# Operands loaded units ahead, gates moved to the end of their phase, attention steps lengthened, first two units interleaved

## The chip, the cores and the metric

The kernel runs on one core of one Trainium2 chip. The metric is the device time of one launch in microseconds (us), the median of several runs; less is better.

## The reference

One layer of a hybrid decoder, in float32, on a prompt of 1024 positions and on 8 sequences of 8 new tokens each (1088 rows together), with a model width of 2048:

```
proj = x @ w_in                                  # 2048 -> 84 blocks of 128 columns
gb, gc, h, z_c, q, k, v, z_a, gate_c, gate_a = split(proj)
y_c = silu(z_c) * gb * short_conv(gc * h)        # 3 taps along the sequence
o   = window attention of q over k, v            # 16 heads of 64, 4 key heads, window 128,
                                                 # ALiBi slopes, a sink logit for each head
y_a = silu(z_a) * o
merged = sigmoid(gate_c) * (y_c @ w_conv_out) + sigmoid(gate_a) * (y_a @ w_attn_out)
y = layer_norm(2**0.25 * x + merged @ w_out) * ln_g + ln_b
```

It also returns the last 128 rows of keys and values and the last two rows of the convolution's input, for the prompt and for each sequence (there after the cached ones).

## The kernel before, in words

**Units.** Activations lie transposed, as tiles of 128 features by T = 1088 rows, of which the first 64 are the new tokens. `w_in` and the two merge projections are multiplied by a 2 x 2 block scheme with seven products. Such a multiplication is cut into units (`unit`, L194): one unit takes a quarter-million weights (a tile `wr` of 128 x 4 x 512, 1024 KB) and 8 tiles of features, and makes two tiles of 128 x 1088. It has 7 products; a product is 4 slices of 6 matmuls (128 x 272), since every operand is kept as a pair: a value rounded to fp32r (ACT) and the rest (DVE subtraction), both made by `split` (L129). A product needs a weight operand (`ready`, L203; some are sums of two blocks) and four operand tiles, kept in a ring of 28 slots (`slot`, L142; 7 steps of 4). Its result goes from PSUM into a tile `c` (`take`, L222): a copy on ACT or an addition on DVE. After each slice `tick` (L92) advances a clock of steps; a unit is 28 ticks. Other PE work is put between the slices: `at` (L88) notes a function for a tick.

**Operands.** `operands` (L148) loads the four quarters of four pairs of feature tiles (16 loads of 272 KB), makes the sums on DVE (L174, L176, L183, L186) and splits all 28 operand tiles (`xa`, `xb`, `xm` in the profile). Each set replaces the one before it in the ring.

**Stages.** (1) 42 units a0 to a41 with the upper half of x's features, their results spilled to DRAM (`pd`). (2) 42 units b with the lower half, which add to the spilled result: two for keys and values (b0, b1), eight for queries and attention gates (b2 to b9; `queries`, L336, and `attend`, L441), eight gates (b10 to b17) beside the attention of the new tokens (`sample`, L508), then eight times two conv units (b26 to b41; `conv`, L605) with one gate each (b18 to b25). `gate` (L462) is a unit, a sigmoid of its whole result and a store to `sgd`. (3) 8 units with conv outputs (m0_0 to m0_7) and 8 with attention outputs (m1_0 to m1_7), multiplied by the gates (`sg`) and added up (`cmo`); the profile names both psm_0 to psm_7. (4) The product with `w_out` in plain matmuls (`o`): 5 row blocks by 4 column blocks by 16 k-steps, then 4 row blocks, with residual and layer norm.

**Attention.** 64 steps (`Step`, L357; 8 pairs of heads by 8 blocks), one in 15 ticks, lie in the slices from b3 on. A step has four parts at fixed ticks after its start (L446 to L449): `load`, 14 ticks later `scores` (matmuls `sc`, then the softmax on DVE and ACT), 11 ticks after that `turn` (four transposes `pt`, then a split into `pp`), 9 ticks after that `output` (matmuls `po`). All three take a PSUM bank of the two tagged `ax` (`aux`, L126). The new tokens' attention has such ticks too (L589 to L593).

**Order.** PE's instructions are chained in program order (`in_order`, L99). On the other engines, and on SP, which issues all DMAs, the framework's planner orders the instructions when the program is built, by times that it simulates; it may pull an instruction ahead of earlier ones as far as its data and buffers allow. `tc.keep_in_program_order` holds one instruction behind whatever was traced before it on its engine. A pool's memory can be used by a later pool when the tiles that lay there are released.

**Output.** After the last merge unit, five `w_out` tiles are loaded into the units' weight buffers (`early`, L692); then the units' pool is closed and the pool `out` takes its memory, with the other raw weights (`wraw`), the raw merged rows (`yr`), the split rows of the new tokens (`ms`) and 8 more slots. `Out.load` (L748) loads the residual rows.

Of the kernel before, what the change touches and what calls it, by code (L numbers as in the profile page):

```python
# [50 lines left out]
def tile_hybrid_step(  # L51
# [8 lines left out]
    def pool(name, bufs=1, space=None, stack=None):  # L60
        kw = {} if space is None else {"space": space}
        if space is not DRAM:
            kw["reuse_waits"] = "tile"
        return (stack or ctx).enter_context(tc.tile_pool(name=name, bufs=bufs, **kw))
# [4 lines left out]
    ps = pool("ps", space=PSUM)  # L69
# [78 lines left out]
    def operands(stage, name, sources):  # L148

        out = [[None] * 4 for _ in range(7)]
        raws = []
        for k, (top, bottom) in enumerate(sources):
            raw = stage.tile([P, 2, T], F32, name=f"xr{name}{k}", tag=f"xr{k}")
            raws.append(raw)
        for h in range(2):
            for r in range(2):
                for raw, src in zip(raws, sources):  # L160
                    c = slice(h * HALF, (h + 1) * HALF)
                    nc.sync.dma_start(raw[:, r, c], src[r][:, c])
        left, right = slice(0, HALF), slice(HALF, T)

        def put(i, src):
            for k in range(4):
                o = slot([2, HALF], F32R, f"x{name}{i}_{k}")
                split(o[:, 0], o[:, 1], src(k))
                out[i][k] = o


        t2 = []
        for k, x in enumerate(raws):
            nc.vector.tensor_sub(x[:, 0, right], x[:, 1, right], x[:, 0, right])  # L174
            t = stage.tile([P, HALF], F32, name=f"t{name}{k}", tag=f"t{k}")
            nc.vector.tensor_add(t, x[:, 0, right], x[:, 0, left])  # L176
            t2.append(t)
        put(0, lambda k: raws[k][:, 0, left])
        put(1, lambda k: raws[k][:, 1, left])
        put(2, lambda k: t2[k])  # L180
        put(3, lambda k: raws[k][:, 0, right])
        for k, x in enumerate(raws):
            nc.vector.tensor_sub(x[:, 0, left], x[:, 1, right], t2[k])  # L183
        put(4, lambda k: raws[k][:, 0, left])
        for k, x in enumerate(raws):
            nc.vector.tensor_sub(x[:, 1, left], x[:, 1, left], t2[k])  # L186
        put(5, lambda k: raws[k][:, 1, left])
        put(6, lambda k: raws[k][:, 1, right])
        return out
# [5 lines left out]
    def unit(name, src, x, c, add):  # L195

        raw = upool.tile([P, 4, 512], F32, name=f"wr{name}", tag="wr", bufs=2)
        nc.sync.dma_start(raw.rearrange("p a b -> p (a b)"), src)
        a11, a21, a12, a22 = (raw[:, i] for i in range(4))
        s = upool.tile([P, 2, 512], F32, name=f"ws{name}", tag="ws", bufs=1)  # L200
# [14 lines left out]
        acc_a, acc_c, acc_b = sums(f"ps{name}")  # L215
# [17 lines left out]
        for i in range(7):  # L233
# [13 lines left out]
            take(*after[i])  # L247


    with ExitStack() as st:  # L250
        stage = pool("stage", stack=st)

        idle = stage.tile([P, HALF], F32, name="idle", tag="t0")
        nc.vector.memset(idle, 0.0)
        t = aux("idle")
        for i in range(WARM):
            matmul(t, idle[:, 0:P], idle[:, 0:512], start=True, stop=True)
        x0 = operands(stage, "a", [(xt[k], xt[k + 8]) for k in range(4)])
        for p in range(len(PAIRS)):
            c = upool.tile([P, 2, T], F32, name=f"ca{p}", tag="c", bufs=2)  # L260
            unit(f"a{p}", win[p, 0], x0, c, False)
            nc.sync.dma_start(pd[p], c)
        x1 = operands(stage, "b", [(xt[k], xt[k + 8]) for k in range(4, 8)])
# [31 lines left out]
    def project(p):  # L295
        c = upool.tile([P, 2, T], F32, name=f"cb{p}", tag="c", bufs=2)
        nc.sync.dma_start(c, pd[p])
        unit(f"b{p}", win[p, 1], x1, c, True)
        return c

    ap = pool("attn", stack=keep)
    kv_ready = {}
# [54 lines left out]
    class Step:  # L357
# [9 lines left out]
        def load(self):  # L367
# [6 lines left out]
            nc.sync.dma_start(self.ks[:, : self.nk].bitcast(F32), ksd[self.g][:, self.lo : self.lo + self.nk])  # L374
            self.vc = ap.tile([P, 2, P], F32R, name=f"vt{n}", tag="vt", bufs=2)
# [65 lines left out]
    def attend(j):  # L441
        t0 = max(clock[0] + 1, attend_from[0])
        for blk in range(NB):
# [4 lines left out]
            at(t + 25, s.turn)  # L448
            at(t + 34, s.output)  # L449
# [3 lines left out]

    with ExitStack() as st:
        sp = pool("heads", stack=st)
        for i in range(2):
            keys_values(i, project(KV + i), sp)
# [4 lines left out]
    def gate(d):  # L462
        c = project(GT + d)
        nc.scalar.activation(c, c, AF.Sigmoid)
        nc.sync.dma_start(sgd[d], c)


    with ExitStack() as st:
# [39 lines left out]
        def sample(g, hb):  # L508
# [5 lines left out]
            sbias = sp.tile([32, L], F32, name=f"sbias{n}", tag="sbias")  # L514
            nc.sync.dma_start(sbias, sbias_d[:, g])
            kt = sp.tile([HD, NH, L], F32, name=f"skt{n}", tag="skt")
# [5 lines left out]
            va = sp.tile([P, NH, HD], F32, name=f"sva{n}", tag="sva")  # L522
# [431 lines left out]
```

## Time and profile before

| | us |
|---|---|
| median of 3 runs | 2820.47 |
| lowest and highest | 2820.05, 2821.55 |
| the profiled execution | 2821.96 |
| its span, from the first instruction to the last | 2820.1 |
| mean granted TensorE clock | 0.971 |

The profile is of one execution. A row of a group reads: line, engine, operation, output<-inputs by the program's names, shapes, count; then busy us and the mean ns of one; then the idle time of the engine just before such instructions and what ended it. PE is TensorE's matmuls, PEld its weight loads, DVE VectorE, ACT ScalarE, SPq the queue of SP that issues DMAs. In the list of waits a row says who waited for whom, us in total, how many times, and the longest. In the timeline a row begins with its start and its duration, and ends, in brackets, with the idle time before it. L110 and L113 are the helpers of all matmuls and transposes, L130 and L131 the two halves of `split`, L227 the additions into `c`.

### The profile page before, as it was taken

What the parts mean: (1) busy time and instruction counts of PE and PEld (TensorE: products, weight loads), DVE (VectorE), ACT (ScalarE), POOL (GpSimd) and SP (SyncE); (2) the same over time, 40 slices, a digit from 0 to 9 for tenths busy, and PEclk for the clock granted to TensorE, in tenths of its full rate; (3) what the DMA queues carried; (4) which work ended last, traced back from release to release, by engine and by line L of the source; (5) the groups of instructions that cost most, each with busy time, mean ns of one, the idle gap of its engine ahead of it and who ended that gap; (6) DMA issues with size and microseconds to landing.
All of it is one profiled execution on the core that took longest, in us unless ns stands there. A gap on an engine that the chain in (4) does not pass through costs nothing.

```text
span 2820.1 us, 47966 instructions
## 1 busy us (share of the span) xinstructions
PE 2660.1 (94%) x19426; PEld 2563.4 (91%) x19426; DVE 1756.9 (62%) x3311; ACT 1072.5 (38%) x2050; POOL 0.2 (0%) x4
## 2 busy tenths in 40 slices
PE   6999999999999989899999999999899999699998
PEld 5999999999999989798999999889899999578886
DVE  7444444444445767687877777777875866433736
ACT  4323323233234445456545444443433422322221
POOL 0000000000000000000000000000000000000000
PEclk8999999999999999899999999999999999899999
DMA  5222222222223456654544444433454366823533
GB/s 202 93 109 108 95 108 107 99 106 106 102 106 118 164 172 198 189 190 149 189 132 155 162 155 143 156 131 129 172 198 165 128 216 214 263 91 109 186 116 105
DMA packets 165026, 411.53 MB, mean 146 GB/s; under 512 B 23186, under 2 KB 75410, under 8 KB 136868
## 3 DMA queue, kind: packets, MB, share of 16 engines
q1 hardware_dynamic: 164804, 408.46, 42.6%
q8 instruction: 153, 2.51, 0.4%
q14 instruction: 69, 0.57, 0.1%
HBM read 290.88 MB, written 119.48 MB: 146 GB/s over the span
## 4 chain that ended last, share of the span: by engine, by line
PE 76%; DVE 12%; DMA 5%; ACT 4%; issue 3%; SPq 0%; DVEq 0%; ACTq 0%
PE o L110 13%; DVE cb L227 2%; DVE wb L131 1%; DMA sg<-sgd 1%; PE pt L113 1%; PE psm_4a L110 1%; PE psm_2a L110 1%; PE psm_5a L110 1%; DMA cmo<-cmd 1%; PE sc L110 1%; ACT p L412 1%; PE psm_0a L110 1%; DVE xm L131 1%; PE po L110 1%; PE psm_6a L110 1%
## 5 line engine op out<-in xcount | busy, mean ns | idle before, releaser
L110 PE MATMUL o<-wo,m 128*128 128x512 f32 x1344 | 319.9, 393 | 0.2 <-DVE r L767 0.2
L110 PEld LDWEIGHTS o<-wo,m 128*128 128x128 f32 x1344 | 254.1, 189 | 55.6 <-issue 0.6
L131 DVE TENSOR_TENSOR wa<-wra,wa 128x512 fp32r<-128x512 f32 x210 | 145.2, 692 | 214.7 <-ACT wa L130 214.7
L130 ACT CAST wb<-wrb 128x512 fp32r<-128x512 f32 x210 | 129.8, 618 | 270.6 <-PE psb3b L110 8.3
L130 ACT CAST wa<-wra 128x512 fp32r<-128x512 f32 x210 | 130.9, 624 | 175.9 <-PE psa0b L110 2.4
L131 DVE TENSOR_TENSOR wo<-wraw,wo 128x512 fp32r<-128x512 f32 x107 | 73.1, 686 | 146.0 <-ACT wo L130 138.4
L131 DVE TENSOR_TENSOR wb<-wrb,wb 128x512 fp32r<-128x512 f32 x210 | 143.7, 684 | 8.6 <-ACT wb L130 8.1
L130 ACT CAST wo<-wraw 128x512 fp32r<-128x512 f32 x107 | 66.2, 621 | 214.4 <-PE o L110 197.1
L131 DVE TENSOR_TENSOR wa<-wsa,wa 128x512 fp32r<-128x512 f32 x84 | 58.1, 692 | 115.2 <-ACT wa L130 115.2
L113 PE MATMUL pt<-ident,p 128*128 128x128 f32 x240 | 47.8, 305 | 50.9 <-ACT p L412 49.8
L130 ACT CAST wb<-wsb 128x512 fp32r<-128x512 f32 x84 | 52.0, 619 | 96.9 <-PE psb18a L110 6.5
L113 PEld LDWEIGHTS pt<-ident,p 128*128 128x128 f32 x240 | 29.9, 148 | 62.0 <-ACT p L412 61.8
L130 ACT CAST wa<-wsa 128x512 fp32r<-128x512 f32 x84 | 52.3, 623 | 78.9 <-issue 76.9
L405 ACT ACTIVATE p<-p,nm 128x256 f32<-128x256 f32 (+1 forms) x128 | 62.4, 488 | 40.9 <-DVE nm L397 40.6
L676 DVE TENSOR_TENSOR cm<-cm,sg 128x544 f32<-128x544 f32 x64 | 46.1, 721 | 49.1 <-DMA sg<-sgd 29.8
L131 DVE TENSOR_TENSOR pp<-pt,pp 128x512 fp32r<-128x512 f32 (+1 forms) x64 | 41.8, 653 | 55.8 <-ACT pp L130 55.7
L131 DVE TENSOR_TENSOR wm<-wrm,wm 128x512 fp32r<-128x512 f32 x80 | 55.0, 687 | 33.3 <-ACT wm L130 33.2
L130 ACT CAST wm<-wrm 128x512 fp32r<-128x512 f32 x80 | 49.8, 622 | 65.7 <-PE psm_0b L110 4.8
L412 ACT ACTIVATE p<-p,den 128x256 f32<-128x256 f32 (+1 forms) x128 | 56.4, 488 | 38.8 <-DVE den L410 38.0
L110 PE MATMUL o<-wo,ms 128*128 128x512 f32 x128 | 40.2, 396 | 28.0 <-DVE ms L131 25.4
L131 DVE TENSOR_TENSOR wb<-wsb,wb 128x512 fp32r<-128x512 f32 x84 | 57.7, 687 | 2.3 <-ACT wb L130 1.9
L110 PEld LDWEIGHTS o<-wo,ms 128*128 128x128 f32 x128 | 24.1, 191 | 33.9 <-issue 27.8
(1089 smaller groups left out, 6582.5 us busy)
## 6 DMA issues: line engine op xcount, KB each, us to landing
pd<-ca SPq DMA_DIRECT2D x42, 1088.0 KB
cb<-pd SPq DMA_DIRECT2D x42, 1088.0 KB
wra<-in_win SPq DMA_DIRECT2D x42, 1024.0 KB
wrb<-in_win SPq DMA_DIRECT2D x42, 1024.0 KB
wraw<-in_wo SPq DMA_DIRECT2D x123, 256.0 KB
sgd<-cb SPq DMA_DIRECT2D x16, 1088.0 KB
sg<-sgd SPq DMA_DIRECT2D x64, 272.0 KB
qt<-qd SPq DMA_DIRECT2D x128, 128.0 KB
```

Of the source, the lines that this page charges most:

```text
L110: in_order(nc.tensor.matmul(*args, **kw))
L113: in_order(nc.tensor.transpose(*args))
L130: nc.scalar.copy(hi, raw)
L131: nc.vector.tensor_sub(lo, raw, hi.bitcast(F32))
L227: nc.vector.tensor_add(dst, dst, val)
L405: nc.scalar.activation(p[:, e, :nk], p[:, e, :nk], AF.Exp, bias=nm[:, e : e + 1], accum_out=den[:, e : e + 1],)
L412: nc.scalar.mul(p[:, e, :nk], p[:, e, :nk], den[:, e : e + 1])
L676: nc.vector.tensor_mul(c[:, f, hs], c[:, f, hs], sg)
```

## The change

*Start and operands.* `operands` becomes a class with separate parts: `load_all` (four loads for each quarter, held in program order), `combine` (the first eight sums), and `step(i)`, which makes the operands of product i only. A unit becomes a generator, `products`, that stops after each product; `enter` runs a set's seven steps, each followed by that product of one or more units. The first two units run side by side with one set, their weights loaded between the quarters, in a PSUM pool of their own of eight banks.

*Hand-overs.* The second set (`x1`) is loaded and combined after unit a36, and its steps are interleaved with b0. The set for conv outputs is loaded and combined before the last three gates, that for attention outputs after the fifth merge unit; both are entered step by step.

*Order of gates.* Nine gates lie beside the new tokens' attention, one after every second conv pair, three after all. A gate's sigmoid is made in two halves.

*Attention.* `turn` comes 16 ticks after `scores`, `output` 10 after `turn`; values and the attention gate are loaded 28 ticks after the step's start. The new tokens' steps come later by 4 to 8 ticks, with two buffers for three of their tiles.

*Output.* `sg` has three buffers. Raw weights and raw merged rows of the output lie in a pool of their own (`mq`), opened after m1_0; the early weights go. The residual loads are held in program order.

```diff
+    class Operands:
+        def load(self, r, c, tag):
+            out = []
+            for k, src in enumerate(self.sources):
+                t = self.stage.tile([P, HALF], F32, name=f"x{tag}{self.name}{k}{r}{c}", tag=f"x{tag}{k}")
+                tc.keep_in_program_order(
+                    nc.sync.dma_start(t, src[r][:, c * HALF : (c + 1) * HALF])
+                )
+                out.append(t)
+            return out
+
+        def load_all(self, between=lambda: None):
+            self.b11 = self.load(0, 0, "a")
+            between()
+            self.b21 = self.load(1, 0, "d")
+            between()
+            self.b22 = self.load(1, 1, "c")
+            self.b12 = self.load(0, 1, "b")
+
+        def combine(self):
+            self.t3, self.t2 = self.b12, self.b22
+            for k in range(4):
+                nc.vector.tensor_sub(self.t3[k], self.t2[k], self.t3[k])
+                nc.vector.tensor_add(self.t2[k], self.t3[k], self.b11[k])
+            self.b22 = None
...
+        def step(self, i):
+            if i == 2 and self.b22:
+                self.combine()
+            if i == 4:
+                for k in range(4):
+                    nc.vector.tensor_sub(self.t3[k], self.b22[k], self.t2[k])
+            if i == 5:
+                for k in range(4):
+                    nc.vector.tensor_sub(self.b21[k], self.b21[k], self.t2[k])
+            self.put(
+                i,
+                (lambda: self.b11, lambda: self.b21, lambda: self.t2, lambda: self.t3,
+                 lambda: self.t3, lambda: self.b21, lambda: self.b22)[i](),
+            )
+            if i == 3:
+                self.b22 = self.load(1, 1, "a")
+
+    def enter(x, *units):
+        for i in range(7):
+            x.step(i)
+            for u in units:
+                next(u)
...
+        x0.load_all(first_weights)
+        s1 = fpool.tile([P, 2, 512], F32, name="wsa1", tag="idle")
+        both = [
+            products(f"a{p}", raws[p], x0.x, c[p], False, (acc[2 * p], acc[2 * p + 1], acc[2 * p + 1]), (None, s1)[p])
+            for p in range(2)
+        ]
+        enter(x0, *both)
...
+    for p in range(2, len(PAIRS)):
+        c = upool.tile([P, 2, T], F32, name=f"ca{p}", tag="c", bufs=2)
+        unit(f"a{p}", win[p, 0], x0.x, c, False)
+        nc.sync.dma_start(pd[p], c)
+        if p == 36:
+            x1.load_all()
+            x1.combine()
...
-            at(t + 25, s.turn)
-            at(t + 34, s.output)
+            at(t + 28, s.load_values)
+            at(t + 30, s.turn)
+            at(t + 40, s.output)
...
-        nc.scalar.activation(c, c, AF.Sigmoid)
+        for f in range(2):
+            nc.scalar.activation(c[:, f], c[:, f], AF.Sigmoid)
...
-            at(t0 + 6, lambda: scores(0))
-            at(t0 + 9, lambda: scores(2))
-            at(t0 + 13, softmax)
-            at(t0 + 20, turn)
-            at(t0 + 25, output)
+            at(t0 + 10, lambda: scores(0))
+            at(t0 + 13, lambda: scores(2))
+            at(t0 + 17, softmax)
+            at(t0 + 26, turn)
+            at(t0 + 33, output)
...
+        gate(8)
...
-            gate(8 + ct)
+            if ct % 2:
+                gate(9 + ct // 2)
...
+    x = branch(0)
+    for d in range(13, 16):
+        gate(d)
...
+    for b, w in enumerate((wc, wa)):
+        for i in range(8):
+            c = upool.tile([P, 2, T], F32, name=f"cm{b}_{i}", tag="c", bufs=2)
+            u = products(f"m{b}_{i}", w[i], x.x, c, False)
+            if i == 0:
+                enter(x, u)
+            else:
+                for _ in u:
+                    pass
+            if (b, i) == (1, 0):
+                st.close()
+                mq = pool("oraw", side="right")
+            merged(b, i, c)
+            if (b, i) == (0, 4):
+                nxt = branch(1)
+        x = nxt
...
-            nc.sync.dma_start(self.r[n][: self.rows], self.x[:, n * 512 : (n + 1) * 512])
+            tc.keep_in_program_order(
+                nc.sync.dma_start(self.r[n][: self.rows], self.x[:, n * 512 : (n + 1) * 512])
+            )
```

`branch(b)` makes a set from `yd`, loads it and combines it. `merged` is the loop of gates and sums that stood in the merge before.

More of the change, by code (lines that the diff above doesn't have):

```diff
@@ new lines, in enter, with unit, products @@
+    def enter(x, *units):
[3 more added lines that the diff above has]
+                next(u)
+        for u in units:
+            assert next(u, None) is None
+    def unit(*args):
+        for _ in products(*args):
+            pass
+    def products(name, src, x, c, add, accs=None, s=None):
+        if len(src.shape) == 3:
+            raw = src
+        else:
+            raw = upool.tile([P, 4, 512], F32, name=f"wr{name}", tag="wr", bufs=2)
+            nc.sync.dma_start(raw.rearrange("p a b -> p (a b)"), src)
@@ L247, in unit, with first_weights @@
             take(*after[i])
-    with ExitStack() as st:
-        stage = pool("stage", stack=st)
-        idle = stage.tile([P, HALF], F32, name="idle", tag="t0")
+            yield
+    st = ExitStack()
+    stage = pool("stage", stack=st, side="right")
+    x0 = Operands(stage, "a", [(xt[k], xt[k + 8]) for k in range(4)])
+    with ExitStack() as first:
+        ps0 = pool("ps0", space=PSUM, stack=first)
+        fpool = pool("first", stack=first, side="right")
+        acc = [ps0.tile([P, 2, 512], F32, name=f"first{i}", tag=f"first{i}") for i in range(4)]
+        idle = fpool.tile([P, 2, 512], F32, name="idle", tag="idle")
         nc.vector.memset(idle, 0.0)
-        t = aux("idle")
         for i in range(WARM):
[L257 to L263, printed above, removed]
+            matmul(acc[0][:, 0], idle[:, 0, 0:P], idle[:, 0], start=True, stop=True)
+        c = [upool.tile([P, 2, T], F32, name=f"ca{p}", tag="c", bufs=2) for p in range(2)]
+        raws = []
+        def first_weights():
+            p = len(raws)
+            raws.append(upool.tile([P, 4, 512], F32, name=f"wra{p}", tag="wr", bufs=2))
+            nc.sync.dma_start(raws[p].rearrange("p a b -> p (a b)"), win[p, 0])
+        x0.load_all(first_weights)
[5 more added lines that the diff above has]
+        enter(x0, *both)
+        for p in range(2):
+            nc.sync.dma_start(pd[p], c[p])
+    ps = pool("ps", space=PSUM)
+    x1 = Operands(stage, "b", [(xt[k], xt[k + 8]) for k in range(4, 8)])
+    for p in range(2, len(PAIRS)):
[5 more added lines that the diff above has]
+            x1.combine()
     keep = ExitStack()
@@ new lines, in tile_hybrid_step, with branch, merged @@
+    mp = pool("merge", side="right")
+    st = ExitStack()
+    stage = pool("mstage", stack=st, side="right")
+    def branch(b):
+        x = Operands(stage, f"m{b}", [(yd[8 * b + k], yd[8 * b + k + 4]) for k in range(4)])
+        x.load_all()
+        x.combine()
+        return x
+    x = branch(0)
+    for d in range(13, 16):
+        gate(d)
+    def merged(b, i, c):
+        for f in range(2):
+            for h in range(2):
+                hs = slice(h * HALF, (h + 1) * HALF)
+                sg = mp.tile([P, HALF], F32, name=f"sg{b}_{i}_{f}{h}", tag="sg", bufs=3)
+                nc.sync.dma_start(sg, sgd[i + 8 * f][:, b, hs])
+                nc.vector.tensor_mul(c[:, f, hs], c[:, f, hs], sg)
+                if b:
+                    sg = mp.tile([P, HALF], F32, name=f"cmo{i}_{f}{h}", tag="sg", bufs=3)
+                    nc.sync.dma_start(sg, cmd[i][:, f, hs])
+                    nc.vector.tensor_add(c[:, f, hs], c[:, f, hs], sg)
+        nc.sync.dma_start((mgd if b else cmd)[i], c)
```

119 lines of the change are left out of this document (35 added, 84 removed).

## The prediction

> **What bounds the kernel now.** I read the page's head first, then the list of what TensorE (PE) waited for, then the busy times in the stretches between the kernel's stages.
>
> ```profile
> span 2820.1 us, 47966 instructions
> PE 2660.1 (94%) x19426; PEld 2563.4 (91%) x19426; DVE 1756.9 (62%) x3311; ACT 1072.5 (38%) x2050; POOL 0.2 (0%) x4
> ```
>
> PE sets the time, so only its gaps and its slow spells can be won: 160 us without a matmul. The list of waits says who ended them:
>
> ```profile
> engine line waited for: us in total, times, longest us
> PE pt L113 <- ACT p L412: 49.8, 24, 4.5
> PE o L110 <- DVE ms L131: 25.4, 2, 24.6
> PE psa0a L110 <- ACT wa L130: 13.4, 1, 13.4
> PE sps L110 <- DMA skt<-in_ckt: 7.4, 1, 7.4
> PE pko L113 <- DVE o L435: 3.1, 1, 3.1
> PE psb3a L110 <- DVE cb L227: 2.8, 1, 2.8
> PE sc L110 <- DMA qt<-qd: 2.5, 1, 2.5
> ```
>
> A unit is 7 products of 24 matmuls, and a product at full clock takes 3.01 us (row below), so a unit takes 21.1 us; 843.7 us for the 40 units a1 to a40 says 21.09.
>
> ```profile
> 88.65 3.01 PE psa2a L110 x24
> ```
>
> The stretches end where the units end. Columns: us, then busy us (instructions) of PE, its weight loads, DVE and ACT, POOL, the granted clock, the DMA share.
>
> ```profile
> 0.00:55.50 55.50, 30.03 (x174) 26.99 (x175) 47.59 (x76) 26.58 (x43) 0.20 (x4) 0.75 0.61 218
> 55.50:899.20 843.70, 843.70 (x6722) 843.70 (x6722) 383.49 (x560) 256.33 (x440) 0.00 (x0) 1.00 0.27 104
> 899.20:927.30 28.10, 23.49 (x171) 23.27 (x170) 26.86 (x43) 21.36 (x39) 0.00 (x0) 0.88 0.32 117
> 992.50:2029.40 1036.90, 968.34 (x7449) 946.25 (x7448) 784.93 (x1765) 508.66 (x1072) 0.00 (x0) 0.97 0.49 161
> 2029.40:2066.40 37.00, 24.51 (x170) 23.11 (x170) 34.85 (x56) 19.20 (x31) 0.00 (x0) 0.82 0.54 201
> 2193.00:2221.00 28.00, 23.26 (x170) 23.04 (x170) 27.34 (x44) 21.55 (x38) 0.00 (x0) 0.88 0.36 117
> 2221.00:2394.00 173.00, 170.00 (x1345) 168.79 (x1343) 115.46 (x179) 51.71 (x89) 0.00 (x0) 1.00 0.63 202
> 2394.00:2430.00 36.00, 11.20 (x43) 8.85 (x42) 8.83 (x16) 5.40 (x12) 0.00 (x0) 0.67 0.90 302
> 2430.00:2808.70 378.70, 373.77 (x1670) 307.87 (x1670) 196.33 (x367) 97.94 (x174) 0.00 (x0) 1.00 0.42 133
> ```
>
> What each loses beyond its units: **start** 55.5 - 21.1 = 34.4; **first hand-over** (a41) 28.1 - 21.1 = 7.0; **attention and gates** (39 units) 1036.9 - 968.3 = 68.6 idle, and 3% of 1036.9 = 31 by the clock, together 99.7; **second hand-over** (m0_0) 37.0 - 21.1 = 15.9; **third** (m0_7, m1_0's operands) 28.0 - 21.1 = 6.9, and 173.0 - 8 x 21.09 = 4.3 in the eight units behind it; **out hand-over** 36.0 less 43 matmuls at 378.7 / 1670 = 0.227 us, so 26.2. In all 194.5 us; the change touches each of these.
>
> **The change, part by part.** *Start.* Today 16 operand loads go ahead of the first weights, and the operands of all seven steps are split before the second weight:
>
> ```profile
> GB/s 0 189 396 335 382 380 402 373 370 418 426 421 273 11 0 0 0 0 0 0 15 295 353 107 308 335 251 335 221 65 322 228 412 389 48 0 0 6 458 289
> 10.14 1.10 SPq L198 DMA_DIRECT2D wra<-in_win  x2
> 27.24 0.60 DVE wa L131
> 27.84 2.54 DVE xa L131 x4
> ```
>
> The first row is the DMA rate in slices of 1.5 us: about 0.39 MB/us from 1.5 us on. The new order is four quarter loads (B11, 1.11 MB), weight 0 (1.05), B21, weight 1, B22, B12. They land near 4.4, 7.0, 9.9, 12.6, 15.5 and 18.3 us, plus half a microsecond. The first matmul comes near 8.5 (after one cast and one subtraction of 0.6 us), the second unit's near 14, and four products bring PE to about 23-24. From 16.7 (first B12 tile) DVE has the eight sums, 20 operand splits and eight later sums at 2.54/4 = 0.635 (22.9 us), 10 weight splits and 4 weight sums at 0.60 (8.4) and 6 additions into c at 0.635 (3.8): 35.1 us, so it is done at 52 and the last two products at 56.5. Today unit a1 ends at 76.6. Gain 20. Below 53 it can't end (12 products behind 17 us), and with DVE's present disorder it would be 65: gain 12 to 24. Two units share one operand step, so DVE has 6 us of matmuls to hide 4 to 7.5 us in, instead of 3; that is the cover, and DVE is late next.
>
> *The first hand-over.* The loads are not what is late:
>
> ```profile
> 30.41 15.12 SPq L162 DMA_DIRECT2D xrb<-in_xt  x15
> ```
>
> The planner has already put them at 30 us. The 28 splits wait for slots that a41 frees product by product. DVE's work between the end of a41's first product and b0's last is 28 splits and 8 sums (36 x 0.635 = 22.9) and about 16 us of the two units' own, 39 us in 36 us of products. So some 3 us stay, whatever the order: gain 4 (0 to 7). The moved loads now issue behind a36's store: 16 issues at about 0.6 us are 9 us of SP's queue and 4.45 MB are 11.4 us of DMA. What queues behind them is a38's weights, needed a unit (21 us) later; without that cover it would cost up to 10 us. The eight sums moved with them (5 us of DVE) fall where DVE is busy 383 of 844 us: nothing.
>
> *Second and third.* The three last gates, 63 us, now hide the loads of conv outputs, which today start after the last gate's work has begun:
>
> ```profile
> 2016.25 11.67 SPq L162 DMA_DIRECT2D xrm<-yd  x16
> ```
>
> With loads and first sums gone the same 3.5 us of DVE excess stays: 15.9 - 3.5 = 12 gained (0 to 15.9). At the third, the loads come four units early; of 6.9 + 4.3 = 11.2 us some 5 stay, as the merge adds DVE work: 6 gained (0 to 11). The third `sg` buffer goes with this.
>
> *Attention.* A turn waits for the softmax. One such step:
>
> ```profile
> 1442.60 0.65 PE L110 MATMUL sc<-kt,qt 128*128 128x256 f32 x4
> 1444.60 2.42 PE L110 MATMUL psb27c<-xb,wb 128*128 128x272 f32 x18
> 1446.85 0.63 PE L110 MATMUL po<-pp,vt 128*128 128x256 f32 x4
> 1450.04 0.57 DVE L435 TENSOR_TENSOR o<-po,ot 64x128 f32<-64x128 f32 x2
> 1456.10 1.30 PE L113 MATMUL pt<-ident,p 128*128 128x128 f32 x4 [4.10 <-ACT p L412]
> 1485.19 0.95 PE L113 MATMUL pt<-ident,p 128*128 128x128 f32 x4 [2.11 <-ACT p L412]
> 1487.05 3.64 PE L110 MATMUL psb18a<-xb,wb 128*128 128x272 f32 x18
> ```
>
> Scores start at 1442.60 and PE could turn 9.4 us later, but the softmax takes 13.5. The turn moves from 11 to 16 ticks behind the scores, a tick being 6 matmuls (3.01/4 = 0.75 us): 3.8 us, and another 0.5 for the next step's scores now ahead of it. The longest wait is 4.5, so of 49.8 us at most 24 x 0.2 = 5 stay if the softmax comes no later. The clock comes back with them: after a wait of 2.11 us 18 matmuls took 3.64 us against 2.42. The sample scores come 4 ticks later, taking 3.0 of the 7.4 us. What stays: sample cache 4.4, pko 3.1, the first step's 2.8 and 2.5, together 13; 6 for turns behind DVE bursts or a PSUM bank; 6 of clock: 25 of 99.7, gain 74. Values and szt are now loaded 28 ticks into a step but 12 ticks (9 us) ahead of their use. All eight conv steps now lie beside attention, so DVE has its 785 us in some 960: 82% instead of 76%. Two half sigmoids for one cost more table loads:
>
> ```profile
> L464 ACT ACT_TABLE_LOAD x14 | 18.0, 1283 | 0.3
> ```
>
> With an exponential between the halves that is two more loads for each of 16 gates, 41 us of ACT at most, which is busy 509 of 1037 and hides it; in one softmax it is 1.3 us of the 4.3 won. Bounds of this stage: 20 (DVE keeps the chain late) to 90.
>
> *Out hand-over.* Today the last merged block waits behind residual loads that the planner pulled ahead, and everything for the output waits behind that block's store:
>
> ```profile
> 2394.91 6.18 DMA r<-in_x_p
> 2401.15 5.67 DMA cmo<-cmd
> 2418.64 10.42 DMA yr<-mgd
> ```
>
> Pinned residuals take the 6.2 out; raw operands and raw weights lie in a pool of their own on the other side, and may come during m1. The first 14 of 16 k-steps don't need the last block and are 14 x 14 matmuls x 0.227 = 44 us of cover for its store. What can be late next is `ms`, still in the pool that takes the units' memory. I take 6 of 26.2 left: gain 20 (0 to 25).
>
> Sum: 20 + 4 + 74 + 12 + 6 + 20 = **136 us**. The profiled execution took 2821.96 us, 1.9 beyond its span, and the median of the runs is 2820.47: 2822 - 136 = 2686, on the median's scale **2684**.
>
> **The rivals.**
> *DVE stays behind in attention.* For: at 1442 to 1455 the softmax is late because conv's work stands ahead of it in DVE's order, and conv steps now come in pairs with no gate between. Against: on the whole DVE has a fifth of the time free. Half of the 74 lost: 2684 + 37 = **2721**.
> *The output still waits for the last block's store*, through `ms`: 20 lost, **2704**.
> *Early operands do nothing*: all three operand hand-overs are DVE's work, not loads, as the row at 30.41 shows for the first. 4 + 12 + 6 = 22 lost: **2706**.
> *Short waits leave the clock alone.* By the row at 1487.05 a wait of 2.1 us already costs 1.2 us more. If only waits of over 3.4 us did, the 6 us of clock that I leave in attention and some 2 elsewhere would go: **2676**.
> The Trainium skill ("TensorE: Matmul & The Clock Gate", the section on the HAM clock gate) has that rule: the clock halves after about one idle window of 3.4 us. By that rule the time would be this rival's; the row at 1487.05 speaks against it.
> *Slower: the PSUM bank.* Scores, turn and output share two `ax` banks. A turn now takes the bank of the output that ran 5 ticks before it (today no bank is taken again within 9 ticks): 3.8 us, and 1 for that output and the scores between. In the step shown the bank was free 3.8 us after the output began (1450.61 - 1446.85); one of the later ones is
>
> ```profile
> 1392.30 0.40 PE L110 MATMUL po<-pp,vt 128*128 128x256 f32 x2
> 1397.14 0.58 DVE L435 TENSOR_TENSOR o<-po,ot 64x128 f32<-64x128 f32 x2 [0.23 <-ACT ot L432]
> ```
>
> 5.4 us, so 0.6 of wait. It decides when every one of 64 steps loses 136/64 = 2.1 us, with 1 of clock in it, that is, when banks come free some 6 us after the output on average; at 7 us it is 64 x (2.2 + 1.2) = 218 lost against 136 won: **2902**.
>
> **How the numbers follow.** Forecast 0.57, DVE 0.17, output 0.10, clock 0.07, no help at hand-overs 0.05, bank 0.04. The forecast alone, by its unknown costs, lies between 2645 and 2715. The range is **2645 to 2735**: the cases at 2676, 2704, 2706 and 2721 lie in it, with room for DVE's to cost a third more than half; out of it fall the bank (0.04) and some 0.05 at either end. A measurement of this kernel tells 0.2% (5.6 us) from no change. All cases but the bank lie over 80 us on the fast side; milder forms of the bank case could meet zero. Faster 0.95, same 0.01, slower 0.04.
>
> **What would show it.** Right: a2 starts near 57; PE's waits on ACT p L412 sum to under 8 us, and the attention stretch has a clock of 0.99; m0_0 and m1_0 take under 26 us; the first output matmul comes within 8 us of the last merge product. Wrong: a wait of pt on DVE o (the bank); den late although pt was moved (DVE); o on ms for over 15 us (the store); many waits of PE on c's additions at L227's successor, which would put DVE ahead of PE as the bound.

## The result and the profile after

| | kernel before | changed kernel |
|---|---|---|
| median, four runs each | 2821.01 us | 2730.85 us |
| lowest and highest | 2820.05, 2826.04 | 2727.61, 2732.11 |
| ratio, 95% interval | | 0.9675 [0.9658, 0.9692] |
| profiled execution, span | 2820.1 | 2728.5 |

The change takes 3.25% off. The forecast was 2684, so two thirds of the 136 us came: the span fell by 91.6. The head of the page after:

```profile
span 2728.5 us, 48044 instructions
PE 2635.7 (97%) x19426; PEld 2546.2 (93%) x19426; DVE 1751.0 (64%) x3311; ACT 1076.7 (39%) x2070; POOL 0.2 (0%) x4
```

To see where they came from, I divided both spans at the same units: where a2 begins, and where b0, b25, m0_0 and m1_7 end. These are the busy times by stretch, first of the kernel before (columns as in the prediction):

```profile
0.00:76.40 76.40, 50.93 (x340) 47.89 (x341) 57.16 (x90) 32.98 (x54) 0.20 (x4) 0.82 0.52 187
76.40:948.60 872.20, 867.57 (x6892) 867.16 (x6891) 416.47 (x615) 278.13 (x479) 0.00 (x0) 1.00 0.28 106
948.60:2029.40 1080.80, 1012.24 (x7801) 990.15 (x7800) 816.57 (x1813) 526.84 (x1106) 0.00 (x0) 0.97 0.49 163
2066.40:2394.00 327.60, 319.86 (x2521) 318.43 (x2519) 219.25 (x338) 111.67 (x193) 0.00 (x0) 0.99 0.56 181
2394.00:2820.10 426.10, 384.98 (x1713) 316.72 (x1712) 212.59 (x400) 103.64 (x187) 0.00 (x0) 0.96 0.45 146
```

and then of the changed kernel:

```profile
0.00:70.20 70.20, 53.53 (x340) 49.43 (x341) 52.37 (x84) 32.93 (x54) 0.20 (x4) 0.88 0.42 153
70.20:942.60 872.40, 866.99 (x6892) 866.58 (x6891) 421.22 (x621) 277.61 (x479) 0.00 (x0) 1.00 0.30 112
942.60:1974.10 1031.50, 990.91 (x7801) 975.02 (x7800) 827.93 (x1843) 543.49 (x1145) 0.00 (x0) 0.99 0.53 174
1974.10:1995.20 21.10, 21.10 (x171) 21.10 (x170) 17.36 (x28) 7.88 (x14) 0.00 (x0) 1.00 0.35 130
1995.20:2315.40 320.20, 317.15 (x2521) 316.32 (x2519) 222.56 (x341) 113.17 (x196) 0.00 (x0) 1.00 0.60 202
2315.40:2728.50 413.10, 386.04 (x1713) 317.75 (x1712) 209.53 (x396) 101.62 (x184) 0.00 (x0) 0.97 0.46 147
```

The second hand-over of the kernel before (m0_0, 37.0 us) is quoted in the prediction. The differences row by row, with attention and the second hand-over as one because the loss moved from one into the other:

| stage | forecast gain | measured gain |
|---|---|---|
| start, to a2 | 20 | 76.4 - 70.2 = 6.2 |
| a2 to the end of b0 (first hand-over) | 4 | 872.2 - 872.4 = -0.2 |
| attention and second hand-over | 74 + 12 | 1080.8 + 37.0 - 1031.5 - 21.1 = 65.2 |
| third hand-over and merge | 6 | 327.6 - 320.2 = 7.4 |
| output | 20 | 426.1 - 413.1 = 13.0 |
| sum | 136 | 91.6 |

Within the 65.2, the first merge unit m0_0 now runs without a stop, but the last gate b25 before it takes 28.8 us, where a unit takes 21.1 and b25 took 22.0 before. Counting the 7.7 over a unit as moved out of the 15.9, the second hand-over gained 8.2 and attention 57.0. What PE waited for, in the changed kernel (rows of the list: who waited, for whom, us in total, times, longest):

```profile
PE o L111 <- DVE ms L132: 10.7, 2, 7.8
PE first L111 <- DVE xa L132: 8.4, 3, 6.2
PE sps L111 <- DMA skt<-in_ckt: 6.5, 1, 6.5
PE pt L114 <- ACT p L480: 6.1, 5, 1.9
PE sc L111 <- DMA qt<-qd: 5.9, 1, 5.9
PE sc L111 <- ACT so L652: 2.5, 1, 2.5
```

The wait that led the list before, 49.8 us of transposes for the softmax, is down to 6.1. No wait over 8 us is left. On top stand two that the forecast had taken for nearly gone: the output on `ms`, and the first operands.

**The start.** Rows of PE and DVE in the changed kernel while step 2 (the third product) begins:

```profile
26.62 0.51 PE L111 MATMUL first<-xa,wa 128*128 128x272 f32 x2 [1.31 <-ACT xa L131]
33.28 1.73 PE L111 MATMUL first<-xa,wa 128*128 128x272 f32 x6 [6.15 <-DVE xa L132]
39.01 3.31 PE L111 MATMUL first<-xa,wa 128*128 128x272 f32 x13 [2.09 <-DVE xa L132]
```

```profile
29.37 0.73 DVE L132 TENSOR_TENSOR xa<-xba,xa 128x544 fp32r<-128x544 f32 x1
30.63 0.73 DVE L132 TENSOR_TENSOR xa<-xba,xa 128x544 fp32r<-128x544 f32 x1
31.87 0.73 DVE L202 TENSOR_TENSOR xda<-xda,xca 128x544 f32<-128x544 f32 x1
32.50 0.73 DVE L132 TENSOR_TENSOR xa<-xca,xa 128x544 fp32r<-128x544 f32 x1
33.14 0.73 DVE L202 TENSOR_TENSOR xda<-xda,xca 128x544 f32<-128x544 f32 x1
33.77 0.73 DVE L199 TENSOR_TENSOR xba<-xaa,xca 128x544 f32<-128x544 f32 x1
```

L132 with input `xca` makes what the third product is waiting for (step 2). The rows with input `xba` are operands of step 3, and L202 and L199 make the sums of steps 5 and 4. They stand ahead of these rows and between them, because the planner, which orders DVE by the times that it simulates, put them there. `step(i)` fixed the order in the program; nothing fixed it on the engine.

**The output.** First rows of SP's queue in the changed kernel, where m1_7 ends at 2315.4, and what SP waited for there; then DVE:

```profile
2322.95 0.32 SPq L762 DMA_DIRECT2D mgd<-cm  x1
2328.86 0.33 SPq L905 DMA_DIRECT2D gB<-in_ln_g  x1
2329.76 1.56 SPq L801 DMA_DIRECT2D yr<-mgd  x3
```

```profile
SPq L905 <- DMA mgd<-cm: 5.5, 1, 5.5
```

```profile
2320.12 0.73 DVE L757 TENSOR_TENSOR cm<-cm,sg 128x544 f32<-128x544 f32 x1 [0.79 <-DMA sg<-sgd]
2322.20 0.72 DVE L761 TENSOR_TENSOR cm<-cm,cmo 128x544 f32<-128x544 f32 x1 [1.35 <-DMA cmo<-cmd]
2322.85 0.49 DVE L132 TENSOR_TENSOR ms<-yr,ms 128x64 fp32r<-128x64 f32 x3
```

The first output matmul waits for three small subtractions into `ms`, 0.49 us together, which stand behind the gating of the last merged block (L757, L761). Until they have run, the three `yr` buffers stay taken and the next `yr` loads, behind the `gB` load in SP's queue, can't be issued. The `gB` load itself (L905) waits 5.5 us for the store of that last block (L762), so the second wait on `ms`, 3.0 us, does hang on the store.

### The profile page after: what moved, and what is told of

Its sections match the earlier page's. It is cut to its first block, busy times and chain, and to the rows that moved or that the text cites. A ratio compares the mean times of both kernels' runs of the same rounds, so it can differ in the third digit from the quotient of the medians.

```text
span 2728.5 us, 48044 instructions
## 1 busy us (share of the span) xinstructions
PE 2635.7 (97%) x19426; PEld 2546.2 (93%) x19426; DVE 1751.0 (64%) x3311; ACT 1076.7 (39%) x2070; POOL 0.2 (0%) x4
## 5 line engine op out<-in xcount | busy, mean ns | idle before, releaser
L132 DVE TENSOR_TENSOR wa<-wra,wa 128x512 fp32r<-128x512 f32 x210 | 145.4, 693 | 216.1 <-ACT wa L131 216.1
L131 ACT CAST wb<-wrb 128x512 fp32r<-128x512 f32 x210 | 129.7, 619 | 247.9 <-PE psb3b L111 12.1
L132 DVE TENSOR_TENSOR wo<-wraw,wo 128x512 fp32r<-128x512 f32 x112 | 76.7, 687 | 148.7 <-ACT wo L131 148.6
L132 DVE TENSOR_TENSOR wb<-wrb,wb 128x512 fp32r<-128x512 f32 x210 | 144.4, 688 | 10.1 <-ACT wb L131 9.1
L132 DVE TENSOR_TENSOR wa<-wsa,wa 128x512 fp32r<-128x512 f32 x84 | 58.2, 693 | 109.9 <-ACT wa L131 109.9
L132 DVE TENSOR_TENSOR wm<-wrm,wm 128x512 fp32r<-128x512 f32 x80 | 55.3, 693 | 39.8 <-ACT wm L131 39.5
L111 PEld LDWEIGHTS first<-xa,wa 128*128 128x128 f32 x336 | 48.2, 212 | 17.7 <-DVE xa L132 9.3
L111 PE MATMUL first<-xa,wa 128*128 128x272 f32 x336 | 49.9, 314 | 14.7 <-DVE xa L132 8.4
L757 DVE TENSOR_TENSOR cm<-cm,sg 128x544 f32<-128x544 f32 x64 | 46.1, 723 | 27.6 <-ACT cm L262 20.3
L132 DVE TENSOR_TENSOR wb<-wsb,wb 128x512 fp32r<-128x512 f32 x84 | 57.6, 686 | 9.1 <-ACT wb L131 9.0
L131 ACT CAST pp<-pt 128x512 fp32r<-128x512 f32 (+1 forms) x64 | 35.8, 560 | 59.1 <-PE pt L114 58.5
L459 DVE SCALAR_TENSOR_TENSOR p<-delta,sc 128x256 f32<-128x256 f32 (+1 forms) x128 | 45.7, 397 | 13.4 <-PE sc L111 13.4
```

The lines of the kernel that those rows point to most:

```text
L111: in_order(nc.tensor.matmul(*args, **kw))
L131: nc.scalar.copy(hi, raw)
L132: nc.vector.tensor_sub(lo, raw, hi.bitcast(F32))
L459: nc.vector.scalar_tensor_tensor(p[:, e, :nk], delta[:, 2 * P - nk :], SLOPES[2 * j + e], sc[:, e, :nk], op0=ALU.mult, op1=ALU.add,)
L757: nc.vector.tensor_mul(c[:, f, hs], c[:, f, hs], sg)
```

## The experiments

Each kernel is the changed one with one edit, except where it says otherwise. The kernel before took 2825.2 us beside the first four, 2831.8 beside the next four and 2824.5 (nine runs) beside the last four, so a single time is good to some 5 us; where less is at stake I read the stage itself. A stage scatters too: from the end of b0 to the end of b24 the changed kernel and five whose edits don't touch that part (`ms` moved, either chain of vector work, first units apart, loads unpinned) take 999.9 to 1006.7 us.

### The old ticks in the changed kernel

```diff
-            at(t + 28, s.load_values)
-            at(t + 30, s.turn)
-            at(t + 40, s.output)
+            at(t, s.load_values)
+            at(t + 25, s.turn)
+            at(t + 34, s.output)
```

> The changed kernel with the attention parts at their old ticks (turn 25, output 34, values loaded with the rest at 0), all else as changed. Theory: the longer steps brought nearly all of the attention stretch's gain, so PE's waits of pt on ACT p come back from 6 us to 40 or more, the clock there falls to 0.97, and the span grows by 45 to 55 us, to 2775 to 2785. Rival: the new order of gates and conv units and the planner's new order on DVE brought half of it or more; then the span grows by 25 us at most, to under 2755.

2808.27 us, span 2806.4: 78 longer than with the new ticks. Its longest wait:

```profile
PE pt L114 <- ACT p L480: 66.7, 26, 8.2
```

More than theory or rival had said. The stretch from the end of b0 to the end of b25 takes 2051.7 - 941.9 = 1109.8 us, against 1080.8 in the kernel before: without the longer steps the rest of the change makes this stretch 29 us slower. 5.4 of them are b25 (27.4 against 22.0); why the turns wait longer than in the kernel before (8.2 against 4.5 at most), the runs don't show.

### The new ticks in the kernel before

```diff
-            at(t + 25, s.turn)
-            at(t + 34, s.output)
+            at(t + 30, s.turn)
+            at(t + 40, s.output)
```

> The kernel before, with one thing changed: the turn of an attention step at its tick 30 instead of 25 and its output at tick 40 instead of 34 (values still loaded at tick 0). Theory (the longer steps work by themselves, by giving the softmax time): the waits of the second transposes for the softmax's result, 49.8 us in the kernel before, fall under 10, and the time goes to 2755-2785 (40 to 70 less than 2825). Rival (they only win back what the new places of the gates and the paired convolution cost, since taking them out of the changed kernel cost 78): under 25 less than before, 2800 or more.

2758.12 us, a span of 2756.3: 63.8 less than the 2820.1 of the kernel before, by two numbers (73.7 by the times, against the 2831.8 beside it). The theory held. The wait, and the same stretch of attention as above (948.6:2029.4 before):

```profile
PE pt L113 <- ACT p L412: 4.6, 4, 2.0
```

```profile
948.40:1966.30 1017.90, 988.92 (x7801) 973.24 (x7800) 811.43 (x1813) 525.36 (x1106) 0.00 (x0) 0.99 0.52 173
```

1080.8 - 1017.9 = 62.9 us, all of it in attention. The whole change gets 49.3 there (1080.8 - 1031.5), so its other edits cost 13.6 in this stretch. 6.8 of them are the growth of b25 (28.8 against 22.0 us), which m0_0 pays back; the next experiment tells these from the rest.

### The last gates among the convolution again

```diff
-            if ct % 2:
-                gate(9 + ct // 2)
+            if ct:
+                gate(8 + ct)
...
-    for d in range(13, 16):
-        gate(d)
```

> The changed kernel with the last gates among the convolution steps again (one behind each of the steps 1 to 7) instead of one behind every second step and three at the end; the loads and first sums for the merge then come straight before it. Theory (the three gates at the end hide these loads, and that is worth the 8.2 us of the second hand-over and a little more): the first merge unit takes 33-38 us instead of 21.1, the last projection unit before it 23-25 instead of 28.8, the time 8 to 14 more, 2738-2744; the convolution stretch, which lost only 8 us, gives back 4 at most. Rival (gates spread out leave the vector engine more room, which the ticks alone, worth 64 in the kernel before, would fit): attention gains 10 or more, and the time is 2730 or less.

2737.29 us, 7.0 more by the spans: a little under the 8 to 14 of the theory, and near the 8.2 read from the two traces. Attention to the end of b25, then m0_0:

```profile
939.10:1961.90 1022.80, 992.98 (x7800) 977.80 (x7799) 810.95 (x1814) 538.85 (x1130) 0.00 (x0) 0.98 0.52 172
1961.90:2000.70 38.80, 26.66 (x171) 25.41 (x170) 35.49 (x56) 18.88 (x31) 0.00 (x0) 0.74 0.40 144
```

m0_0 is back at 38.8, with 12.1 us of waits on `xm` from DVE. The gates at the end buy 38.8 - 21.1 = 17.7 and pay 1031.5 - 1022.8 = 8.7, of which b25 is 6.8; the rival's 10 us in attention didn't come. The 1022.8 are still 4.9 more than with the ticks alone (1017.9), in a stretch that holds the same units: what else the change does to attention (two buffers and later ticks for the new tokens, values loaded later, split sigmoids) shows no gain there, and 4.9 is within the scatter of such a stretch.

### Vector work in program order: the first set, then all four

Every DVE instruction of a set (sums and low halves) gets an order dependency on the one traced before it; nothing else is moved. The condition on the name stands in the first of the two kernels only. `last_operand` starts as `[None]`, and `on_dve` also wraps the sums for steps 4 and 5 and those of `combine`.

```diff
+    def chained(ins):
+        if last_operand[0] is not None:
+            tc.add_manual_dep(ins.ins, last_operand[0].ins.name,
+                mybir.DependencyInfo(mybir.DependencyClass.NoSync, mybir.DependencyReason.DATA),
+                reason="chained")
+        last_operand[0] = ins
...
+        def on_dve(self, ins):
+            if self.name == "a":
+                chained(ins)
...
-                split(o[:, 0], o[:, 1], src[k])
+                nc.scalar.copy(o[:, 0], src[k])
+                self.on_dve(nc.vector.tensor_sub(o[:, 1], src[k], o[:, 0].bitcast(F32)))
```

> The changed kernel with DVE's instructions on the first operand set (sums and low halves) held in the order of the program among themselves. Theory: the start gained 6 us and not 20 because the planner placed sums and splits of products 4 to 7 ahead of the second to fourth operand tile of product 3; with the order held a2 begins at 58 to 63 us instead of 70.2 and the span falls by 7 to 12 us. Rival: the last quarters land too late for anything else; then a2 still begins at 68 or later.

> The same order held for all four operand sets. Theory: at the hand-overs into b0, m0 and m1 DVE has 3 to 4 us more to do than PE, so the units a41 and b0 together still lose 4 us or more and the last gate and m0_0 too. Rival: there too it was the planner's order; then each of these losses (7.4 and 7.7 us in the changed kernel) falls under 3 us, and the span falls by 8 us or more beyond the run with the first set alone.

First set alone: 2727.53 us, a2 begins at 62.2 as the theory had it; the span falls by 2.7 only, not by 7 to 12. All sets: 2715.59 us, span 2713.8, 14.7 less; a2 begins at 61.2, a41 and b0 take 21.1 + 26.3 us (before the edit 23.4 + 26.2) and b25 24.7 (28.8). PE at the same place as above, with all sets chained:

```profile
23.79 0.79 PE L111 MATMUL first<-xa,wa 128*128 128x272 f32 x5
29.27 12.96 PE L111 MATMUL first<-xa,wa 128*128 128x272 f32 x86 [4.68 <-DVE xa L204]
```

One wait of 4.7 us in place of three with 9.6, and no stop after it. So the planner's order cost 8 to 9 us at the start and some 6 at the first two hand-overs. The 4.7 that remain are the eight sums ahead of the third product, and 5.2 of b0 and 3.6 of b25 over 21.1 remain too, so theory and rival each held in part. In b25 DVE is busy for 24.3 of 24.8 us: there its work is the bound, not its order. In b0 it is busy for 22.3 of 26.4, with 3.2 us of waits and a granted clock of 0.94; what holds b0 stays open.

The first kernel's span fell by only 2.7 of the 8.0 that the start gained. The rest went in stages that the edit doesn't touch, the largest part in b10. Below b10 with the first set chained; in the changed kernel it was the second row's:

```profile
1155.75:1193.20 37.45, 30.41 (x205) 28.75 (x203) 26.14 (x76) 16.39 (x43) 0.00 (x0) 0.82 0.66 190
```

```profile
1165.00:1199.70 34.70, 27.61 (x205) 26.32 (x204) 25.92 (x75) 16.01 (x43) 0.00 (x0) 0.90 0.62 179
```

The same 205 matmuls and the same 6.5 us of wait for the keys of the new tokens; only the granted clock differs, and with it 2.8 us: it stood at half for 13.7 us in the first and for 6.8 us in the second.

### `ms` out of the units' memory

```diff
-    ms = op.tile([P, KT, P], F32R, name="ms")
+    ms = mq.tile([P, KT, P], F32R, name="ms", tag="ms")
```

> The changed kernel with the tile ms in the pool of the raw output rows instead of the pool that takes the units' memory. Theory: ms comes late because its memory is released late; its subtraction then stands behind the last merged block on DVE, and the three raw rows' buffers stay taken with it. Then the wait of 7.8 us before the first output matmul falls to under 2 and that of 3.0 behind the third k-step to under 1, and the span falls by 8 to 12 us, to 2716 to 2721. Rival: DVE is held by the loads that the last block's additions wait for, wherever ms lies; then 5 us or more of the first wait stays.

2713.15 us, span 2711.4: 17.1 less, more than the 8 to 12 that were expected. m1_7 ends at 2312.66 and the output's first matmul begins at 2312.50, its queue running without a gap:

```profile
2312.50 0.63 PE L111 MATMUL o<-wo,ms 128*128 128x512 f32 x2
2312.97 2.92 PE L111 MATMUL o<-wo,m 128*128 128x512 f32 x12
```

The output stage takes 2711.4 - 2312.7 = 398.7 instead of 413.1 us, 14.4 less: the two waits of 7.8 and 3.0 on `ms`, and the slow matmuls behind the first, of which the next row is the changed kernel's (4.98 us for what takes 2.92 above; the granted clock stood at half there until 2328.6). The other 2.7 are in stages that the edit doesn't touch.

```profile
2324.20 4.98 PE L111 MATMUL o<-wo,m 128*128 128x512 f32 x12
```

### The residual loads without their pin

```diff
-            tc.keep_in_program_order(
-                nc.sync.dma_start(self.r[n][: self.rows], self.x[:, n * 512 : (n + 1) * 512])
-            )
+            nc.sync.dma_start(self.r[n][: self.rows], self.x[:, n * 512 : (n + 1) * 512])
```

> The changed kernel without the pin that keeps the residual loads of the output in the order of the program. Theory (as forecast: loads pulled ahead stand before the last merged block's operands, 6.2 us in the kernel before): the wait before the first output matmul grows from 7.8 to 13-16, the time by 4 to 8, 2734-2738. Rival (the first output waits on the vector engine and on the buffers of raw operands, not on the transfer queue): no change within 3 us of 2730.

2743.09 us, 12.8 more by the spans, of which 8.9 are in the output stage (422.0 against 413.1). The wait grows as the theory had it:

```profile
PE o L111 <- DVE ms L132: 18.5, 2, 14.7
```

14.7 - 7.8 = 6.9 us are what the pin is worth at this wait; the forecast had 6.2. The time rose by more than the 4 to 8 expected; 3.1 us of it are in b10 (37.5 against 34.4), which the edit doesn't touch.

### Output of an attention step four ticks earlier

```diff
-            at(t + 40, s.output)
+            at(t + 36, s.output)
```

> The changed kernel with the output of an attention step at tick 36 instead of 40, the turn still at 30. Theory (what is left in attention are the waits for banks that the turn and the output of neighbouring steps share, 7.0 us in all): the bank waits fall under 4, and the time by 3 to 5, to 2725-2728. Rival (the output then stands before the copy of the turned softmax is done, as it was with tick 34): new waits of the output for that copy, and 10 to 40 more, 2740-2770.

2723.73 us, 6.6 less by the spans, and 6.5 less in the stretch from the end of b0 to the end of b25 (1025.0 against 1031.5). The waits for `so` and `o`, 7.0 us before (2.5 + 1.9 + 1.6 + 1.0), are down to one over a microsecond, 1.2, beside one of 3.3 before `pko` that came back and waits for `o` as well. The rival's long wait of the output for `pp` didn't come (0.4). To the end of b24 the stretch takes 996.3, which is 3.6 below the lowest of the six above, so not all of the 6.5 is scatter. A part may be chance of position: the wait for the sampled keys fell from 6.5 to 1.9 as well.

### The first steps' data: other memory, a later start

Two edits aim at the waits for the first queries (5.9) and the first sampled keys (6.5).

```diff
-        sp = pool("sample", stack=st)
+        sp = pool("sample", stack=st, side="right")
```

> The changed kernel with the pool of the sampled tokens placed at the other end of the memory, so that its tiles need not wait until the tiles of the heads' phase give their memory back. Theory (the first sampled tokens are late because of memory that is still in use): the wait of the first scores for the transposed keys (6.5 us) and that for the queries (5.9) fall to under 3 together, 8 to 10 less, 2719-2723. Rival (SP's queue stands behind other waits anyway): at least 4 of each stay, within 3 us of 2730.

2729.12 us: 3.5 us of the wait for the keys stay, the queries' stays (6.4), and the time is the same, nearly as the rival had it (at least 4 of each). The sampled tokens' first load is issued 10.2 us after b10 begins (1163.1 in this kernel), against 10.3 before, and SP waits 2.2 us ahead of it in both kernels, for the store of the last queries:

```profile
SPq L587 <- DMA qd<-qb: 2.2, 1, 2.2
```

So the move didn't take that wait away. Why it is still there, the runs don't settle.

```diff
-        t0 = max(clock[0] + 1, attend_from[0])
+        t0 = max(clock[0] + 1, attend_from[0]) + (6 if j == 0 else 0)
...
-            t0 = clock[0]
+            t0 = clock[0] + (6 if n == "0_0" else 0)
```

> The changed kernel with the first attention step, and the first step over the sampled tokens, begun 6 ticks (some 3.5 us of convolution) later, nothing else moved except that all later steps of attention follow by the same 6 ticks. Theory (the data of the first step are stored and loaded back through SP's queue, and the first scores simply come too early): the waits for the queries (5.9 us) and for the sampled keys (6.5 us) fall to under 3 together, and the time by 8 to 12, to 2718-2722. Rival (the loads stand behind other waits of SP's queue, which move along): at least 4 of each stay, and the time within 4 of 2730.

2729.13 us: neither. The queries' wait fell to 2.1 and the keys' went, as the theory had it, but the time stayed, because new waits came with the new positions:

```profile
PE sc L111 <- ACT so L652: 5.1, 1, 5.1
PE sps L111 <- DVE p L459: 4.1, 1, 4.1
```

By this run what is lost in attention now isn't one late load: a shift trades some waits for others.

### The first two units one after the other

```diff
-        enter(x0, *both)
+        enter(x0, both[0])
+        for _ in both[1]:
+            pass
```

> The changed kernel without the pairing of the first two units: the first one's matmuls alone, then the second's. Theory (the interleaving of the first two units gives nearly all of the 6.2 us that the start gained): the third unit begins 5 to 8 later, at 75-78 instead of 70.2, and the time is 2734-2739. Rival (the gain came from the order in which operands are summed, and the pairing holds the first unit back): the third unit begins within 2 us of 70.2 or earlier, time 2726-2732.

2735.89 us, 5.6 more by the spans; a2 begins at 74.7, 4.5 later. Nearly the theory's 5 to 8: of the start's 6.2 us the pairing is worth some 4.5.

### Three edits together

`ms` in its own buffer, all sets chained, output at tick 36.

> The changed kernel with three single edits together: all vector operations of the four operand sets in the order of the program, the low half of the merged blocks in a buffer of its own, and the output of an attention step at tick 36. Theory (each removes its own waits): the gains add, 17 + 15 + 7 = 39 less than 2730, 2688-2696, ratio to the kernel before 0.952 to 0.956. Rival (two of them move the same work on the vector engine, so a wait removed at one place is one found at the next): less than 28 together, 2703 or more.

2693.21 us (five runs, 2691.39 to 2696.25), ratio to the kernel before 0.9535 [0.9522, 0.9548]. The gains add: 17.1 + 14.7 + 6.6 = 38.4 expected from the three spans, 2728.5 - 2689.7 = 38.8 found; that the two agree so closely is chance, by the scatter of a single time. This version beats both kernels. a2 begins at 62.3, and the last stretch is:

```profile
2291.00:2689.70 398.70, 383.05 (x1713) 314.46 (x1711) 204.89 (x382) 97.00 (x169) 0.00 (x0) 0.99 0.45 150
```

## Why the prediction was right, and where it was not

Direction and main mechanism were right, and the time lies inside the range, 4 us from its slow end. That it lies inside is owed to the width of the range: start, attention and output each gained less than forecast, all on one side, and the start less than its own lower bound (6.2 against 12). Of the signs that the prediction named, the waits on ACT p (6.1 us), the clock of attention (0.99), m0_0 and m1_0 (21.1 and 22.0 us) and the first output matmul (7.8 us after the last merge product, just under the 8) came out; a2 at 57 did not. Of the 44 us that are missing, point by point:

- **Start: 14 missing, a failed step.** The prediction counted 35.1 us of DVE from the first B12 tile and took them in the order of the products; "with DVE's present disorder it would be 65" was kept as the other end of the term. The disorder was not a thing of the old code's listing but of the planner, which the new code leaves free: 70.2. With the order forced it is 62.2 and 61.2, so 8 to 9 of the 14 are order. The last 5 are the wait of 4.7 for the eight sums: the prediction had them in DVE's total, but they stand ahead of the third step, when PE has only the four products of the first two steps to run meanwhile.
- **First hand-over: 4 missing.** "Some 3 us stay, whatever the order" failed: 7 stay, and with the order forced 5, of which the runs show 3.2 as waits in b0. The early loads do nothing here, as the rival "early operands do nothing" said for this one place.
- **Second hand-over: 4 missing.** 8.2 by the traces, 7.0 by taking the late gates out. The step "the same 3.5 us of DVE excess stays" was too small by half for the same reason: 7.7 stay with the planner's order, 3.6 with the program's. They stay in b25, a unit earlier than forecast, because the first operands are now split there.
- **Attention: 17 missing, a term that was mis-sized.** The mechanism was right: the longer steps alone give 62.9, and the turns' wait is 6.1 us where the prediction left 5. Of 99.7 the prediction left 25, and 43 stay (99.7 - 57.0). Banks shared by turn and output were put at 6 together with the turns behind DVE; turns alone are 6.1, and the banks 7.0. The first steps' loads, with the additions into c at b3, take 15.7 where 13 were left. Additions into c elsewhere take 4.9, which no term had. The rest, some 9, no wait explains; it is put down to the clock (0.99 over the stretch), where 6 were left. (Banks: the waits for `so` and `o` of 2.5, 1.9, 1.6 and 1.0; additions: 1.7, 1.4, 1.3 and 0.5 at b11, b8, b4 and b32.) The rival "DVE stays behind", priced at 37, describes part of this but not its cause: the softmax did come in time.
- **Slower by the bank: fell.** The banks cost 7 us in all, not 2.1 in each of 64 steps.
- **Two half sigmoids: little on ACT, as said.** Its whole busy time rose by 4.2 us (1072.5 to 1076.7) where up to 41 had been allowed. No run takes this edit alone.
- **Third hand-over: right in size.** 7.4 against 6. No run takes its edits (loads four units early, the third `sg` buffer) apart.
- **Output: 7 missing, the rival named `ms`.** The sentence "what can be late next is `ms`, still in the pool that takes the units' memory" was right, and the price between the two cases: 7 lost, not none and not 20. The first matmul waits behind DVE's gating of the last block, not for that block's store, which is issued only at 2322.95, as the subtractions run. The second wait of 3.0 us hangs on the store after all, through the `gB` load. Of the 13.0 us gained, 8.9 go back without the pin. With `ms` moved the stage has gained 13.0 + 14.4 = 27.4 us, the whole 26.2 and a little more, so the 6 that the prediction left for other causes were not there.
- **The clock.** The rival "short waits leave the clock alone" fell, but the length of a wait alone doesn't decide. Two waits of the changed kernel, and then the busy times in stretches of 3.41 us around them (columns as before, the granted clock behind POOL):

```profile
995.86 3.25 PE L111 MATMUL psb3a<-xb,wb 128*128 128x272 f32 x24 [3.28 <-DVE cb L264]
1631.24 0.95 PE L114 MATMUL pt<-ident,p 128*128 128x128 f32 x4 [1.86 <-ACT p L480]
```

```profile
990.61:994.03 3.42, 1.97 (x16) 1.75 (x14) 3.39 (x7) 2.09 (x3) 0.00 (x0) 1.00 0.44 165
994.03:997.44 3.41, 1.58 (x12) 1.61 (x13) 3.41 (x6) 0.26 (x1) 0.00 (x0) 1.00 0.95 204
997.44:1000.85 3.41, 3.41 (x30) 3.41 (x29) 1.50 (x3) 0.62 (x1) 0.00 (x0) 1.00 0.91 211
1628.91:1632.32 3.41, 1.47 (x11) 1.06 (x10) 2.58 (x10) 1.64 (x5) 0.00 (x0) 1.00 0.69 242
1632.32:1635.73 3.41, 3.41 (x17) 3.41 (x17) 2.14 (x5) 2.46 (x7) 0.00 (x0) 0.50 0.05 15
1635.73:1639.14 3.41, 3.41 (x29) 3.41 (x29) 1.35 (x2) 1.60 (x2) 0.00 (x0) 1.00 0.00 0
```

The bounds of these stretches are the trace's own: the granted clock falls to 0.50 eleven times in it, and the falls begin (at 28.05, 925.76, 1004.27, 1178.35, 1263.68, 1294.40, 1632.32 and so on) whole multiples of 3.413 us apart. The stretch with the wait of 1.86 us held 1.47 us of matmuls, and the next one ran at half clock: 17 matmuls where the one behind it held 29. The wait of 3.28 us lies across the bound at 994.03; its stretches held 1.97 and 1.58 us, and the clock stayed at 1.00. So it counts how much of a wait falls between two bounds. In the fourteen traces of this case, behind the start, every stretch at full clock with under 1.5 us of matmuls was followed by one at half clock and none with over 2.3; in between both occur. The Trainium skill ("TensorE: Matmul & The Clock Gate", the section on the HAM clock gate) states a fall after an idle window of about 3.4 us, and that the window runs freely. The trace bears out the window's length (3.41 us) and the wait of 3.28 us, but not that the whole window must be idle: 1.94 us without a matmul out of 3.41 were enough.

## What to carry to other kernels

Interleaving work in the program text does not interleave it on an engine that a planner orders: look for later steps' instructions between the ones that are waited for, and pin the order there (15 us here). A buffer that is needed first after a stage change should not lie in memory that the stage before gives back last (`ms`, 14 us of the stage for one line). When a dependent chain is late by a fixed amount in many steps, a few ticks more between its parts are the cheapest edit there is: two numbers gave 64 of the 92 us.

## What the runs showed of the hardware that was not expected

The same program part with the same wait took 34.7 and 37.5 us in two kernels that differ only in the first operand set, at a granted clock of 0.90 and 0.82 (b10, above). A wait of 3.28 us cost the clock nothing; one of 1.86 us halved it for the next 3.41 us. What decided was where the wait lay between bounds 3.413 us apart. So the price of a short wait can't be read off its length, and whatever shifts the program shifts it too: in the kernel with the first set chained a gain of 8.0 us at the start was 2.7 at the end, though one run can't tell that from scatter.
